# A macaron encoder block in float32r: 40 + 40 subtractions of the weight and activation splits put on GpSimd instead of VectorE

## The chip, the cores and the metric

The kernel runs on one core of a Trainium2 chip. Its engines work side by side, each through its own queue in order: TensorE (PE in the profile, its weight loads PEld), VectorE (DVE), ScalarE (ACT), GpSimd (POOL), and SyncE (SP), which here issues the DMAs. The metric is device time in microseconds, the median of several runs. The profile is one execution of its own.

## The reference, cut to what matters

One encoder layer over a sequence of 512 tokens with width 1024, all in float32: a feed-forward block, a mixer (gated convolution and mLSTM heads), and a second feed-forward block, each with a norm before and after and a residual. The two feed-forward blocks are what the change touches:

```python
def swiglu(x, w_in, w_out):
    gate, up = jnp.split(x @ w_in, 2, axis=-1)
    return (jax.nn.silu(gate) * up) @ w_out

h = swiglu(rmsnorm(x, norm_ffn1_pre[l]), w_ffn1_in[l], w_ffn1_out[l])
x = x + FFN_RESIDUAL_SCALE * rmsnorm(h, norm_ffn1_post[l])
```

`w_in` is 1024 x 5632 (gate and up factors of 2816 columns each), `w_out` 2816 x 1024.

## The kernel before, in words

**Splits.** TensorE multiplies in float32r, which keeps fewer bits than float32. So each operand is split in two: `hi`, a rounding cast made by ScalarE, and `lo`, the rest `src - hi`, a subtraction made by VectorE. Both lines are in the helper `split` (lines 292 and 294), so all splits of the kernel show up under these two lines and are told apart by tile names and shapes. `split` has a parameter `eng` for the engine of the subtraction, with VectorE as its default. A product takes three matmuls: hi x hi, hi x lo, lo x hi. In the kernel before, GpSimd forms the rests of only the first four weight tiles (`ON_POOL`).

**Seven products.** Both feed-forward projections use a scheme with seven products of half-size blocks in place of eight (with sums and differences of blocks formed first).

**In-projection.** The hidden columns go in 22 steps of 128 (`NF`), `j`. The first two (`PLAIN`) are done plainly, the other 20 by seven products. For such a step `w_pair` (from line 151 on; the additions are line 158) takes the two raw 128 x 1024 weight tiles of a step, gate `g` and up `u`, forms sums and differences in place, and splits four things: `g` (products 1 and 2), `s1` (product 5), the changed `g` (products 6 and 3) and the changed `u` (products 7 and 4). The last of these is the up factor's split. In `ffn` the products of a step are written in the order 1, 5, (4 of the step before), 6, 3, 2, 7; each is 12 matmuls of 256 columns (line 431). Three PSUM banks (`x`, `y`, `z`) hold a step's sums, and between the products ScalarE copies (lines 495 to 506) and VectorE adds (lines 503, 505, 508, 509 and 484) take them out: product 4 adds onto the bank that line 508 has read after product 7. `w_get(1)` keeps one step's weights formed ahead.

**Out-projection.** The 22 row blocks of `w_out` go in the order `OUT`: five groups "a" (`SEVEN` = 5), each over a pair of row blocks, then "b", "k", "b", "k" and so on, then the rest "k". A group "a" does products 1, 5, 6 and 7, a "b" products 2, 3 and 4 (line 564, 6 matmuls of 512 columns for each product), and a "k" is a plain row block (line 589, 24 matmuls).
- `w_out_a` prepares the right sides of an "a": three subtractions of 512 columns (line 191), a split of `r0` (1024 columns: products 1 and 7) and splits of `r1` and `t` (512 each: products 5 and 6).
- `left_a` prepares its left side from the hidden activations `h`: three additions of 256 columns (line 531) and splits of 256, 256 and 512 columns, the last of them for products 7 and 6.
- `w_out_b` and `left_b` do the same for a "b"; product 4's weight there is the split into the tile `wt` (subtraction before it: line 214).
- After the last "a", `taken` moves the sums out of PSUM (ScalarE copies at lines 574 and 576, VectorE additions at line 531), since the banks are used again.

**What sets the order.** The kernel is written in the Tile framework. A planner, which runs the instructions against a timeline of its own before the program is emitted, decides the order within each engine's queue, and inserts the waits. Instructions passed to `pin` keep their written order; in `ffn` that ends for the other engines after the first four plain products, and for TensorE after the first of the seven products. So from there the order of the products, the copies and the splits is the planner's.

**Buffers.** Twelve split tiles of 1024 columns (`wpool`, seven for a step of the in-projection, four for an "a"), four raw weight tiles (`rawp`) that the loads on SyncE's queue fill as they come free, 13 larger tiles (`big`) for activations, eight PSUM banks.

Of the kernel before, what the change touches and what calls it, by code (L numbers as in the profile page):

```python
# [37 lines left out]
def encoder_kernel(ctx: ExitStack, tc: tile.TileContext, a: dict, out: bass.AP):  # L38
    nc = tc.nc
# [14 lines left out]
    def nm(s):  # L54
        uid[0] += 1
        return f"{s}_{uid[0]}"
# [7 lines left out]
    def t2(dt=F32):  # L64
        return t2p.tile([P, 512], dt, tag="t2", name=nm("t2"))

    def t4(dt=F32):
        return t4p.tile([P, 1024], dt, tag="t4", name=nm("t4"))
# [4 lines left out]
    def f32(ap):  # L73
        return ap.bitcast(F32)
# [10 lines left out]
    def pin(ins):  # L85

        if pinned["PE" if ins.ins.engine == nc.tensor.engine else "rest"]:
            tc.keep_in_program_order(ins)
# [62 lines left out]
    def w_pair(g, u):  # L151


        def wt(n):
            return wpool.tile([P, 1024], F32R, tag="w", name=nm(n))

        def add(o, a_, b_, op):
            nc.vector.tensor_tensor(out=o, in0=a_, in1=b_, op=op)  # L158

        c = (slice(0, 512), slice(512, 1024))  # L160
        s1 = t2()
        add(s1, u[:, c[0]], u[:, c[1]], ALU.add)
        add(u[:, c[0]], g[:, c[0]], u[:, c[0]], ALU.subtract)
        gh, gl = wt("whi"), wt("wlo")
        split(gh, gl, g)
        add(g[:, c[0]], s1, g[:, c[0]], ALU.subtract)
        add(g[:, c[1]], g[:, c[1]], g[:, c[0]], ALU.subtract)
        s1w = wt("ws1")
        split(s1w[:, c[0]], s1w[:, c[1]], s1)
        ch_, cl = wt("whi"), wt("wlo")  # L170
        split(ch_, cl, g)
        uh, ul = wt("whi"), wt("wlo")
        split(uh, ul, u)

        def q(h_, l_, a_, b_):
            return tuple(v[:, r].rearrange("p (k f) -> p k f", k=KD // 2) for v, r in ((h_, a_), (l_, b_)))

        return {
            1: q(gh, gl, c[0], c[0]), 2: q(gh, gl, c[1], c[1]), 5: q(s1w, s1w, c[0], c[1]),
            6: q(ch_, cl, c[0], c[0]), 3: q(ch_, cl, c[1], c[1]),  # L180
            7: q(uh, ul, c[0], c[0]), 4: q(uh, ul, c[1], c[1]),
        }
# [3 lines left out]
    def w_out_a(r0, r1):  # L186

        c = (slice(0, 512), slice(512, 1024))

        def sub(o, a_, b_):  # L190
            nc.vector.tensor_tensor(out=o, in0=a_, in1=b_, op=ALU.subtract)

        def wt(n):
            return wpool.tile([P, 1024], F32R, tag="w", name=nm(n))

        sub(r1[:, c[0]], r0[:, c[1]], r0[:, c[0]])
        sub(r0[:, c[1]], r1[:, c[1]], r0[:, c[1]])
        t = t2()
        sub(t, r1[:, c[1]], r1[:, c[0]])
        kept.append(t)  # L200
        ah, al = wt("whi"), wt("wlo")
        split(ah, al, r0)
        bh, bl = wt("whi"), wt("wlo")
        split(bh[:, c[0]], bl[:, c[0]], r1[:, c[0]])
        split(bh[:, c[1]], bl[:, c[1]], t)
        return {1: (ah[:, c[0]], al[:, c[0]]), 7: (ah[:, c[1]], al[:, c[1]]),
                5: (bh[:, c[0]], bl[:, c[0]]), 6: (bh[:, c[1]], bl[:, c[1]])}

    def w_out_b(r1):

        c = (slice(0, 512), slice(512, 1024))
        hi, lo, t = (wpool.tile([P, 1024], F32R, tag="w", name=nm(n)) for n in ("whi", "wlo", "wt"))
        split(hi, lo, r1)
        nc.vector.tensor_tensor(out=r1[:, c[0]], in0=r1[:, c[0]], in1=kept.pop(0), op=ALU.subtract)
        split(t[:, c[0]], t[:, c[1]], r1[:, c[0]])
        return {2: (hi[:, c[0]], lo[:, c[0]]), 3: (hi[:, c[1]], lo[:, c[1]]), 4: (t[:, c[0]], t[:, c[1]])}

    def w_split(n):
        for _ in range(n):
            if not loaded:  # L220
                w_load(1)
            if not loaded:
                return
            raws, kk = loaded.pop(0)
            if isinstance(kk, str):
                ready.append((w_out_a if kk == "a" else w_out_b)(*raws))
                continue
            if len(raws) == 2:
                ready.append(w_pair(*raws))
                continue  # L230
            raw = raws[0]
            hi = wpool.tile([P, 1024], F32R, tag="w", name=nm("whi"))
            lo = wpool.tile([P, 1024], F32R, tag="w", name=nm("wlo"))
            eng = nc.gpsimd if done[0] in ON_POOL else nc.vector
            done[0] += 1
            split(hi, lo, raw, eng)
            if kk > 1:
                hi, lo = (v.rearrange("p (k f) -> p k f", k=kk) for v in (hi, lo))
            ready.append((hi, lo))
# [51 lines left out]
    def split(hi, lo, src, eng=nc.vector):  # L291
        latest["hi"] = nc.scalar.copy(out=hi, in_=src)  # L292
        pin(latest["hi"])
        latest["lo"] = eng.tensor_tensor(out=lo, in0=src, in1=f32(hi), op=ALU.subtract)  # L294
        pin(latest["lo"])
# [139 lines left out]
    def ffn(xq, between, finish, mid=None, within=None, ahead=(2, 2, 1, 1), late=None):  # L435
# [51 lines left out]
        for j in range(PLAIN, NF):  # L487
# [4 lines left out]
            a_, u, c = t2(), t2(), t2()  # L492
# [34 lines left out]
        def hcol(k):  # L527
            return h[k // 4][:, k % 4, 0:512]

        def tt(o, a_, b_, op):  # L530
            nc.vector.tensor_tensor(out=o, in0=a_, in1=b_, op=op)  # L531

        def halves():
            t = bigt(F32R).rearrange("p q f -> p (q f)")
            return t[:, 0:1024], t[:, 1024:2048]

        def parts(hi, lo, at):
            return {n: (hi[:, c:c + 256], lo[:, c:c + 256]) for n, c in at.items()}

        def left_a(i):  # L540
            a_, b_ = hcol(2 * i), hcol(2 * i + 1)
            hi, lo = halves()
            s1 = t4()[:, 0:256]
            tt(s1, a_[:, early], b_[:, early], ALU.add)
            split(hi[:, 0:256], lo[:, 0:256], a_[:, later])
            tt(a_[:, early], a_[:, later], a_[:, early], ALU.subtract)
            tt(a_[:, later], s1, a_[:, later], ALU.subtract)
            split(hi[:, 256:512], lo[:, 256:512], s1)
            split(hi[:, 512:1024], lo[:, 512:1024], a_)
            return parts(hi, lo, {1: 0, 5: 256, 7: 512, 6: 768})  # L550

        def left_b(i):
# [42 lines left out]
        for at, (kind, n) in enumerate(OUT):  # L595
            if kind == "k":
                if plain_n % 2 == 0:
                    hs = bigt(F32R)
                q = 2 * (plain_n % 2)
                plain_n += 1  # L600
                hT = (hs[:, q, 0:512], hs[:, q + 1, 0:512])
                split(hT[0], hT[1], hcol(n))
                ks[n] = (hT, w_get(min(2, len(OUT) - 1 - at)))
                if n == 12 and mid:
                    mid()
                if n < NF - TAIL:
                    for tb in range(NT):
                        for half in range(2):
                            mm_out(tb, half, n, *ks[n])
            elif kind == "a":  # L610
                left, right = left_a(n), w_get(1)
                for m in (1, 5, 6, 7):
                    product_out(m, left, right, n == 0, n == SEVEN - 1)
                    if n == SEVEN - 1:
                        taken(m)
            else:
                left, right = left_b(n), w_get(2)
                for m in (2, 3, 4):
                    product_out(m, left, right, n == 0 and m == 4, False)
# [339 lines left out]
    for tb in range(NT):  # L959
        pv_ = ps()  # L960
        n = 0
        for k in range(KD):
            hi, lo = wv[k // 2]
# [198 lines left out]
```

## Time and profile before

| | |
|---|---|
| median of 3 runs | 918.28 us (918.09 to 918.73) |
| the profiled execution | 915.36 us, span 913.7 us, granted TensorE clock 0.999 |
| PE busy | 900.1 us, 99% of the span |
| DVE busy | 716.2 us, 78% |
| ACT busy | 444.6 us, 49% |
| POOL busy | 44.7 us, 5% |
| DMA | 96.47 MB, mean 106 GB/s |

The first feed-forward block runs from the start to about 342 us (its in-projection to 228 us), the mixer to about 567 us, the second block from there to the end (its in-projection to 783 us). Busy time is an average over stages with different limits; a row of a group gives line, engine, operation, output tile and input tile, shape and count, then the busy time, the mean of one in ns, and the idle time ahead of it with what ended it. A row of the timeline or of the chain gives the start in us from the span's start and the duration. The matmuls' ends are modelled, so their pace is read from starts and counts, not from the duration of one.

### The profile page before, as it was taken

The page shows a single profiled execution, that of the slowest core. Times are in us where ns is not written, and L with a number is a line of the kernel's source. Part 1 is how long each engine was busy: PE and PEld are TensorE (multiplying, and loading weights), DVE is VectorE, ACT ScalarE, POOL GpSimd, SP SyncE. Part 2 cuts the span into 40 slices and gives each one's busy share as a digit, 9 for nine tenths or more (in the row PEclk, how much of TensorE's full clock was granted, in tenths as well). Part 3 has the DMA queues.
Part 4 walks back from the last instruction along what each step waited for, and adds up shares of the span by engine and source line. Part 5 has one row for each costly group of instructions (what it writes and reads, how often), then busy time and mean ns, then how long its engine had stood idle before and what let it go on. Part 6 is the DMA issues. An engine that isn't in the chain of part 4 may idle for free.

```text
span 913.7 us, 15022 instructions
## 1 busy us (share of the span) xinstructions
PE 900.1 (99%) x6015; PEld 816.7 (89%) x6015; DVE 716.2 (78%) x1196; ACT 444.6 (49%) x745; POOL 44.7 (5%) x67
## 2 busy tenths in 40 slices
PE   8999999999999999999999999999999999999997
PEld 7999999999877888987888888999999999977885
DVE  6988998888988359498787746889888988999435
ACT  6655555555456235452434335545545545566311
POOL 5000000000002001000011000000000000000000
PEclk9999999999999999999999999999999999999999
DMA  8233443343335614231422602224343432343402
GB/s 256 68 114 116 119 135 97 102 127 96 93 127 149 199 47 116 63 100 47 116 70 70 197 12 66 74 68 118 112 120 93 118 108 87 119 140 110 162 2 91
DMA packets 126257, 96.47 MB, mean 106 GB/s; under 512 B 4182, under 2 KB 114794, under 8 KB 126187
## 3 DMA queue, kind: packets, MB, share of 16 engines
q1 hardware_dynamic: 126186, 95.51, 35.1%
q8 instruction: 47, 0.77, 0.4%
q14 instruction: 24, 0.19, 0.1%
HBM read 93.40 MB, written 2.10 MB: 105 GB/s over the span
## 4 chain that ended last, share of the span: by engine, by line
PE 93%; DVE 4%; ACT 1%; issue 1%; DMA 1%; SPq 0%; POOL 0%; DVEq 0%; POOLq 0%; ACTq 0%
PE ps L431 43%; PE ps L589 13%; PE ps L422 12%; PE ps L564 9%; PE ps L453 5%; PE ps L1119 5%; PE ps L965 2%; DVE big L294 1%; DVE wlo L294 1%; PE ps L343 1%; DVE big L531 1%; PE ps L1035 1%; DMA x<-in_x_dram 1%; PE ps L983 0%; PE ps L391 0%
## 5 line engine op out<-in xcount | busy, mean ns | idle before, releaser
L294 DVE TENSOR_TENSOR wlo<-raw,whi 128x1024 fp32r<-128x1024 f32 x207 | 245.0, 1192 | 58.9 <-ACT whi L292 44.2
L292 ACT CAST whi<-raw 128x1024 fp32r<-128x1024 f32 x211 | 211.8, 1028 | 145.9 <-DVE raw L158 45.0
L431 PE MATMUL ps<-big,whi 128*128 128x256 f32 x1920 | 264.8, 280 | 0.0
L431 PEld LDWEIGHTS ps<-big,whi 128*128 128x128 f32 x1920 | 243.5, 188 | 0.5
L431 PE MATMUL ps<-big,wlo 128*128 128x256 f32 x960 | 150.9, 280 | 0.0
L431 PEld LDWEIGHTS ps<-big,wlo 128*128 128x128 f32 x960 | 129.3, 188 | 0.0
L589 PE MATMUL ps<-whi,big 128*128 128x512 f32 x384 | 121.9, 395 | 0.2 <-ACT whi L292 0.2
L589 PEld LDWEIGHTS ps<-whi,big 128*128 128x128 f32 x384 | 72.0, 188 | 17.4 <-ACT whi L292 0.6
L422 PE MATMUL ps<-big,whi 128*128 128x512 f32 (+1 forms) x384 | 79.8, 358 | 0.2 <-DVE den L1053 0.2
L564 PE MATMUL ps<-whi,big 128*128 128x512 f32 x240 | 75.9, 395 | 2.6 <-ACT big L292 2.6
L589 PE MATMUL ps<-wlo,big 128*128 128x512 f32 x192 | 75.6, 395 | 0.0
L422 PEld LDWEIGHTS ps<-big,whi 128*128 128x128 f32 x384 | 63.5, 188 | 11.2 <-PE ps L1077 0.4
L431 PE MATMUL ps<-big,ws 128*128 128x256 f32 x480 | 65.3, 280 | 0.0
L431 PEld LDWEIGHTS ps<-big,ws 128*128 128x128 f32 x480 | 60.3, 188 | 0.0
L564 PEld LDWEIGHTS ps<-whi,big 128*128 128x128 f32 x240 | 44.7, 188 | 13.4 <-ACT big L292 3.4
L501 ACT COPY t<-ps 128x256 f32<-128x256 f32 x40 | 14.9, 371 | 72.8 <-PE ps L431 72.7
L292 ACT CAST big<-big 128x512 fp32r<-128x512 f32 (+2 forms) x68 | 36.1, 582 | 23.2 <-DVE big L531 10.8
L564 PE MATMUL ps<-wlo,big 128*128 128x512 f32 x120 | 44.9, 393 | 0.0
L589 PEld LDWEIGHTS ps<-wlo,big 128*128 128x128 f32 x192 | 36.1, 188 | 8.4
L422 PE MATMUL ps<-big,wlo 128*128 128x512 f32 (+1 forms) x192 | 41.1, 356 | 0.0
L294 DVE TENSOR_TENSOR big<-big,big 128x512 fp32r<-128x512 f32 (+2 forms) x68 | 40.7, 634 | 0.1
L422 PEld LDWEIGHTS ps<-big,wlo 128*128 128x128 f32 x192 | 32.1, 188 | 5.5
(212 smaller groups left out, 1143.3 us busy)
## 6 DMA issues: line engine op xcount, KB each, us to landing
raw<-in_w_ffn_in_dram SPq DMA_DIRECT2D x88, 512.0 KB, 4.8
raw<-in_w_ffn_out_dram SPq DMA_DIRECT2D x44, 512.0 KB, 5.0
raw<-in_w_mix_in_dram SPq DMA_DIRECT2D x24, 512.0 KB, 4.5
raw<-in_w_mix_out_dram SPq DMA_DIRECT2D x8, 512.0 KB, 3.6
raw<-in_w_ffn_out_dram SPq DMA_DIRECT2D x10, 256.0 KB, 4.0
out_dram<-x SPq DMA_DIRECT2D x8, 256.0 KB, 2.0
x<-in_x_dram SPq DMA_DIRECT2D x4, 256.0 KB, 4.9
x<-in_x_dram SPq DMA_DIRECT2D x2, 512.0 KB
```

The source lines that it names most:

```text
L292: latest["hi"] = nc.scalar.copy(out=hi, in_=src)
L294: latest["lo"] = eng.tensor_tensor(out=lo, in0=src, in1=f32(hi), op=ALU.subtract)
L343: pin(nc.tensor.transpose(out=pt[:, blk(k)], in_=xs[:, blk(4 * b + k)], identity=ident))
L422: nc.tensor.matmul(o, ww[:, k, :], xk(xT, xx, k, sl), start=n == 0, stop=n == 3 * KD - 1)
L431: pin(nc.tensor.matmul(o, ww[:, k, :], x[xx][:, k, :], start=first and n == 0, stop=n == 11, skip_group_check=True))
L453: pin(nc.tensor.matmul(o, ww[:, k, :], xq_hl(xq, (k // 4, th))[xx][:, k % 4, :], start=n == 0, stop=n == 3 * KD - 1))
L501: nc.scalar.copy(a_[:, h1], x[:, h0])
L531: nc.vector.tensor_tensor(out=o, in0=a_, in1=b_, op=op)
L564: nc.tensor.matmul(acc[tb + t][half], left[n][x][:, blk(t)], right[n][y], start=first and x == y == 0, stop=last_ and x == 1, skip_group_c ...
L589: nc.tensor.matmul(acc[tb][half], hT[hh][:, blk(tb)], w[ww][:, blk(half, 512)], start=fresh and hh == ww == 0, stop=k == NF - 1 and hh == ...
L965: nc.tensor.matmul(pv_, xk(xT, xx, k, blk(tb)), ww[:, k % 2, :], start=n == 0, stop=n == 3 * KD - 1)
L1119: nc.tensor.matmul(acc[half], yy[yi][:, k % 4, blk(tb)], wmo[k][wi][:, blk(half, 512)], start=(n == 0 and yi == 0 and wi == 0), stop=(n == ...
```

## The change

Four places hand `nc.gpsimd` to `split`: the rest of the up factor in `w_pair` (1024 columns, 20 per block), the rests of the weights of products 5 and 6 in `w_out_a` (2 x 512 columns, 5 groups per block) and of product 4 in `w_out_b` (512 columns, 5 per block), and the rest of the left side of products 7 and 6 in `left_a` (512 columns, 5 per block). Over both blocks these are 40 subtractions of 1024 and 40 of 512 columns. Nothing else is edited; the planner runs anew.

```diff
@@ w_pair
         uh, ul = wt("whi"), wt("wlo")
-        split(uh, ul, u)
+        split(uh, ul, u, nc.gpsimd)
@@ w_out_a
         bh, bl = wt("whi"), wt("wlo")
-        split(bh[:, c[0]], bl[:, c[0]], r1[:, c[0]])
-        split(bh[:, c[1]], bl[:, c[1]], t)
+        split(bh[:, c[0]], bl[:, c[0]], r1[:, c[0]], nc.gpsimd)
+        split(bh[:, c[1]], bl[:, c[1]], t, nc.gpsimd)
@@ w_out_b
-        split(t[:, c[0]], t[:, c[1]], r1[:, c[0]])
+        split(t[:, c[0]], t[:, c[1]], r1[:, c[0]], nc.gpsimd)
@@ left_a
             split(hi[:, 256:512], lo[:, 256:512], s1)
-            split(hi[:, 512:1024], lo[:, 512:1024], a_)
+            split(hi[:, 512:1024], lo[:, 512:1024], a_, nc.gpsimd)
```

## Prediction

> **What bounds the kernel now.** I read the page first, then the busy time by stage, then what TensorE waited for, then VectorE's instructions in the stage that looked tight.
>
> ```profile
> span 913.7 us, 15022 instructions
> PE 900.1 (99%) x6015; PEld 816.7 (89%) x6015; DVE 716.2 (78%) x1196; ACT 444.6 (49%) x745; POOL 44.7 (5%) x67
> ```
> ```profile
> 36.00:228.00 192.00, 192.00 (x1634) 192.00 (x1633) 167.69 (x265) 101.45 (x162) 0.00 (x0) 1.00 0.38 110
> 219.80:258.70 38.90, 38.90 (x230) 34.23 (x229) 38.69 (x73) 21.38 (x39) 0.00 (x0) 1.00 0.44 133
> 777.10:815.00 37.90, 37.90 (x214) 32.84 (x214) 37.90 (x72) 21.27 (x40) 0.00 (x0) 1.00 0.44 136
> ```
> ```profile
> PE ps L564 <- ACT big L292: 2.6, 2, 1.3
> ...
> PE ps L564 <- ACT wt L292: 0.9, 1, 0.9
> PE ps L589 <- ACT whi L292: 0.2, 1, 0.2
> ```
> ```profile
> 36.40 192.10 PE ps L431 x1632
> ...
> 862.96 44.52 PE ps L589 x192
> ```
>
> The columns of the second fence are the window, its length, then the busy time (instructions) of PE, PEld, DVE, ACT and POOL, the granted clock, the DMA share and GB/s. The fourth is from the chain that ended last (start, length, count). TensorE is busy throughout 36 to 228 us (the first block's in-projection): 192.10 us for 1632 matmuls of 256 columns is 0.117 us each, and a matmul of 512 columns takes 44.52 / 192 = 0.232 us. VectorE is 87% busy there (167.69 of 192.00), idle 24.3 us; GpSimd does nothing. In the transition to the out-projection (219.8 to 258.7, and 777.1 to 815.0 in the second block) VectorE has no idle time at all, while TensorE is still fed. The third fence, the waits of TensorE (us in total, times, longest), holds all that it lost in the two feed-forward blocks after their start: 2.6 + 0.9 + 0.2 = 3.7 us. So the change can win little, and can lose wherever it makes VectorE or the new GpSimd pieces late.
>
> **What the change is made of.** It adds and removes no arithmetic: 40 subtractions of 1024 columns (the up factor of each of 20 pairs, two blocks) and, per block, 5 x 3 of 512 columns in the "a" groups (weights of products 5 and 6, left side of 6 and 7) and 5 of 512 in the "b" groups (weight of product 4) go from VectorE to GpSimd. ScalarE's rounding casts, DMAs and matmul counts stay. The durations:
>
> ```profile
> L294 POOL TENSOR_TENSOR wlo<-raw,whi 128x1024 fp32r<-128x1024 f32 x4 | 9.6, 2402 | 1.4 <-ACT whi L292 1.3
> ```
> ```profile
> L294 DVE TENSOR_TENSOR wlo<-raw,whi 128x1024 fp32r<-128x1024 f32 x8 | 9.7, 1217 | 0.6 <-ACT whi L292 0.6
> ...
> L294 DVE TENSOR_TENSOR wlo<-t,whi 128x512 fp32r<-128x512 f32 x5 | 3.4, 680 | 0.0
> L294 DVE TENSOR_TENSOR wlo<-raw,whi 128x512 fp32r<-128x512 f32 x5 | 3.4, 680 | 0.0
> L294 DVE TENSOR_TENSOR big<-big,big 128x512 fp32r<-128x512 f32 x5 | 3.4, 679 | 0.0
> ```
> ```profile
> 255.36 0.68 DVE L294 TENSOR_TENSOR wlo<-t,whi 128x512 fp32r<-128x512 f32 x1
> 255.96 0.68 DVE L294 TENSOR_TENSOR big<-big,big 128x512 fp32r<-128x512 f32 x1
> 256.56 1.22 DVE L294 TENSOR_TENSOR wlo<-raw,whi 128x1024 fp32r<-128x1024 f32 x1
> 257.70 0.41 DVE L531 TENSOR_TENSOR big<-big 128x256 f32<-128x256 f32 x1
> ...
> 261.40 1.29 DVE L531 TENSOR_TENSOR big<-ps,big 128x512 f32<-128x512 f32 x2 [2.69 <-PE ps L564]
> ```
>
> Of the second fence (VectorE in 219.8 to 258.7 us) the last three rows are the 15 subtractions of the "a" groups: all lie in the tight stretch. Back to back, VectorE starts the next instruction 0.60 us after one of 512 columns and 1.14 us after one of 1024 (third fence): that is what it is spared. GpSimd takes 2.40 us for 1024 columns; for 512 no row stands, and I estimate half, 1.20 us. If the two engines ran beside each other freely, VectorE would be spared 15 x 0.60 = 9.0 us per tight stretch. Whether they do is the question.
>
> **Do they run beside each other?** Three places say: only when VectorE reads PSUM.
>
> ```profile
> 10.38 4.93 POOL L294 TENSOR_TENSOR wlo<-raw,whi 128x1024 fp32r<-128x1024 f32 x2 [1.27 <-ACT whi L292]
> ```
> ```profile
> 10.47 2.48 DVE L294 TENSOR_TENSOR big<-ps,big 128x512 fp32r<-128x512 f32 x4
> ```
> ```profile
> 458.25 0.64 POOL L1018 TENSOR_SCALAR_AFFINE_SELECT t<-t 128x512 f32<-128x512 f32 x1 [14.08 <-ACT t L1016]
> ```
> ```profile
> 458.47 0.96 DVE L294 TENSOR_TENSOR big<-t,big 128x512 fp32r<-128x512 f32 x1
> ```
> ```profile
> 283.99 0.21 POOL L706 CAST big<-rawg 128x32 fp32r<-128x32 f32 x1 [12.82 <-DMA rawg<-in_w_mix_in_dram]
> ```
> ```profile
> 284.14 1.36 POOL L706 CAST big<-rawg 128x32 fp32r<-128x32 f32 x2
> ```
> ```profile
> 284.18 1.24 DVE L294 TENSOR_TENSOR wlo<-raw,whi 128x1024 fp32r<-128x1024 f32 x1 [0.26 <-ACT whi L292]
> ```
>
> At 10.38 us two GpSimd subtractions ran beside VectorE's, which read one operand from PSUM: four in 2.48 us, the usual 0.6 each. At 458.47 a VectorE subtraction with both operands in SBUF met a GpSimd instruction that began at 458.25: it took 0.96 instead of 0.68 us. GpSimd ended at 458.89; from there to VectorE's end (459.43) are 0.54 us, so VectorE stood still until GpSimd was done. The other way round, two GpSimd casts, of 0.21 us each when alone, ended only at 284.14 + 1.36 = 285.50, just after the VectorE subtraction of 284.18 to 285.42. The two take turns, a whole instruction each.
>
> [...]
>
> **The sum.** In the tight stretches VectorE works without a pause, so what counts is how long each GpSimd subtraction keeps it standing, against 0.60 us spared. Lower bound: it does not stand at all, -0.60 each. The 0.64 us row: +0.04. Upper: 1.20 us, +0.60. I take a hold of 1.20, since it is the same operation's row halved, and that 85% of it blocks:
>
> ```profile
> L484 DVE TENSOR_TENSOR big<-ps,t 128x256 f32<-128x256 f32 x3 | 1.2, 414 | 0.0
> ...
> L503 DVE TENSOR_TENSOR t<-ps,t 128x256 f32<-128x256 f32 x2 | 0.8, 418 | 0.2 <-PE ps L431 0.2
> ...
> L508 DVE TENSOR_TENSOR t<-ps,t 128x256 f32<-128x256 f32 x2 | 0.8, 414 | 0.0
> ...
> L505 DVE TENSOR_TENSOR t<-ps,t 128x256 f32<-128x256 f32 x1 | 0.4, 416 | 0.0
> ```
>
> These 8 instructions read PSUM and may run under a hold: 8 x 0.33 = 2.7 us of the 38.9 - 9.0 = 29.9 that stay, 9%; I round the free share up to 15% for holds that start while VectorE waits for something else. So 1.20 x 0.85 - 0.60 = +0.42 us each, 15 x 0.42 = +6.3 us of VectorE time per block.
>
> What of it reaches TensorE depends on its lead in the last "a" group:
>
> ```profile
> 260.89 1.09 PE L564 MATMUL ps<-whi,big 128*128 128x512 f32 x4
> ```
> ```profile
> 813.46 0.68 DVE L294 TENSOR_TENSOR big<-big,big 128x512 fp32r<-128x512 f32 x1
> ```
> ```profile
> 815.71 1.09 PE L564 MATMUL ps<-whi,big 128*128 128x512 f32 x4
> ```
>
> A group has 4 products x 6 = 24 matmuls, 5.57 us. In the first block the last one ends at 260.89 + 4 x 0.232 = 261.82, so it began at 256.25; VectorE finished its last left rest at 256.64 (255.96 + 0.68), which the second or third product needs (in its third matmul) at 258.1 or 259.5: a lead of 1.5 to 2.9, I take 2.2. In the second block it began at 811.07 and the rest was there at 814.14, for a third product's third matmul at 814.3: a lead of 0.2. So TensorE loses 6.3 - 2.2 = 4.1 and 6.3 - 0.2 = 6.1 us. VectorE's pause of 2.69 us at 261.40 does not help: it lies behind the group that came late, and the matching pause of the second block is shorter.
>
> The "b" groups: the first of them falls into the stretch right behind, where VectorE again has no pause; +0.42 in each block, 0.8 in all. The others cost nothing: a "b" with its "k" group holds 18 + 24 matmuls (9.7 us), about twice the VectorE work that goes with it; without that cover they would cost 8 x 0.42 = 3.4 us.
>
> ```profile
> raw<-in_w_ffn_in_dram SPq DMA_DIRECT2D x88, 512.0 KB, 4.8
> ```
>
> The up factors (a 2.40 us subtraction for 1.14 spared, every 84 x 0.117 = 9.8 us): 20 x (2.40 x 0.85 - 1.14) = +18 us of VectorE time in a 192 us stage that has 24.3 idle. I cost it at nothing: the two weight tiles of a pair are formed a whole pair ahead and the up rests are used by products 7 and 4, the last. Without that cover the bounds are 0 and 20 x (2.40 - 1.14) = 25 us per block. The raw tile is given back up to 2.4 us later, and SyncE's queue with the next load behind it; a load lands in 4.8 us (row above) of the 9.8, so it stays ahead. On GpSimd nothing urgent is queued behind the new work: a wait there holds back only the next subtraction, and the norm's powers come after the blocks. GpSimd's own load is 3 x 1.20 = 3.6 us per "a" group plus up to three waits of 0.6 for a VectorE instruction: 5.4 of TensorE's 5.57, so it is no cushion either.
>
> Sum: 4.1 + 6.1 + 0.8 = +11.0 us. The profiled execution took 915.36 us (its span 913.7 and 1.7 around it), 2.9 below the median of the runs, 918.28. 915.36 + 11.0 = 926.4; on the median, **929.3 us**.
>
> **The rivals.** (1) *Relief, faster.* GpSimd reads in short pieces and lets VectorE through; VectorE ends each tight stretch up to 9 us earlier and TensorE's waits of 3.7 us go. For it: a wait of 0.9 us in the second block has its cast behind VectorE's subtractions. Against: the two of 1.3 us follow casts queued behind ScalarE copies that wait for TensorE itself, and would stay. So -1.1 to -3.7, 914.6 to 917.2 us; it decides if less than half (0.60 / 1.20) of a hold blocks. Chance 0.17. (2) *No change.* Holds fall where VectorE waits anyway, or the planner, which orders each engine's queue, forms the "a" pieces earlier and takes up the stretch: 918.3 us. Against: the second block's lead of 0.2. Chance 0.18. (3) *The in-projection too.* VectorE, at up to (167.7 + 18) / 192 = 97%, falls behind by single holds and empties PSUM late; product 4 may only write after a sum of product 7 has been read. At 0.3 us for each of 38 inner pairs, +11.4 more: 940.7 us. Against: the lead of a whole pair. Chance 0.15.
>
> **How the numbers follow.** Forecast 0.50 (within 921 to 937: both blocks with 0.64 and with 1.20 us fully blocking), rivals as above. What a measurement of this kernel can tell from no change is about 0.2%, 1.8 us. Faster by more: most of rival 1, 0.13. Within: the rest of it, rival 2 and the lowest end of the forecast, 0.22. Slower: 0.65. The range leaves out the lower part of rival 1 and the upper half of rival 3: 915 to 941 us.
>
> **What would show it.** Right: VectorE instructions of 512 columns from SBUF with means well above 0.68 us around the transition; GpSimd about 96 + 48 us busier; new TensorE waits on line 564 released by GpSimd or VectorE, some 4 to 6 us per block; the in-projection still without waits. Wrong: VectorE's durations unchanged beside a busy GpSimd (rival 1), stretched durations but no TensorE wait (rival 2), or waits on line 431 (rival 3). A different order of products on TensorE could make any of these terms wrong.

## The result: 28 us slower, and the profile after

The changed kernel takes 946.21 us (median of 4 runs, 944.24 to 946.77) against 918.18 us for the kernel before: ratio 1.0302 (1.0284 to 1.0320). The prediction had the sign and the two engines' exclusion, 929.3 us, and a range up to 941: too little by 17 us. One of the ten runs of the control among the experiments (e12) took 979.98 us at a granted clock of 0.851 and does not enter its ratio.

The head of the page of the profile after, then its busy times by window (columns as in the prediction: length, PE, PEld, DVE, ACT, POOL, granted clock, DMA share, GB/s), then its longest waits of TensorE (us in total, times, longest):

```profile
span 942.5 us, 15253 instructions
PE 910.6 (97%) x6015; PEld 821.6 (87%) x6015; DVE 736.6 (78%) x1116; ACT 446.8 (47%) x745; POOL 231.9 (25%) x147
```
```profile
38.00:226.00 188.00, 186.24 (x1580) 185.77 (x1579) 167.67 (x236) 97.14 (x152) 45.73 (x19) 1.00 0.37 109
226.00:262.00 36.00, 32.15 (x182) 27.17 (x181) 34.80 (x51) 17.49 (x33) 24.49 (x12) 0.95 0.33 103
262.00:292.00 30.00, 26.09 (x111) 20.64 (x112) 27.68 (x34) 18.47 (x33) 20.22 (x8) 1.00 0.33 100
593.00:795.00 202.00, 201.03 (x1706) 200.62 (x1705) 180.10 (x246) 108.81 (x168) 49.72 (x20) 1.00 0.35 101
795.00:836.00 41.00, 33.99 (x181) 27.67 (x180) 38.75 (x52) 17.11 (x33) 24.31 (x15) 1.00 0.35 107
836.00:870.00 34.00, 28.35 (x113) 22.31 (x112) 25.87 (x39) 20.92 (x37) 15.98 (x4) 0.90 0.31 103
```
```profile
PE ps L564 <- POOL wt L294: 5.6, 2, 4.5
PE ps L564 <- ACT big L292: 4.0, 3, 1.7
PE ps L564 <- DVE wlo L294: 4.0, 2, 2.6
PE ps L564 <- DVE t L503: 3.7, 2, 3.1
PE ps L431 <- DVE t L508: 2.2, 3, 1.2
PE ps L564 <- DVE big L484: 1.9, 1, 1.9
...
PE ps L564 <- POOL big L294: 1.2, 1, 1.2
```

Three things are to be seen. VectorE gave up 80 subtractions and is busier than before, 736.6 against 716.2 us: it stands still inside other instructions (line 158's 40 of `t<-raw` take 1176 ns each on the mean, 684 in the profile before). TensorE's losses lie in the two transitions to the out-projection: in the second and third window it is idle 3.9 + 3.9 us, in the last two 7.0 + 5.7 us; the in-projections lose 1.8 and 1.0. And its clock fell below 1.00 in two of the windows, which no window of the two blocks had before.

The waits name the new releasers: GpSimd itself (`wt`, product 4's weight, and `big`, the left side), and VectorE, late. The moved subtractions on GpSimd, from the groups of the profile after by shape:

```profile
L294 POOL TENSOR_TENSOR wlo<-raw,whi 128x1024 fp32r<-128x1024 f32 x44 | 109.9, 2497 | 313.1 <-ACT whi L292 222.0 <-DVE wlo L294 49.5 <-PE ps L431 41.7
L294 POOL TENSOR_TENSOR wt<-raw,wt 128x512 fp32r<-128x512 f32 x10 | 33.1, 3309 | 35.8 <-ACT wt L292 35.8
L294 POOL TENSOR_TENSOR big<-big,big 128x512 fp32r<-128x512 f32 x10 | 23.8, 2395 | 21.1 <-ACT big L292 21.1
L294 POOL TENSOR_TENSOR wlo<-raw,whi 128x512 fp32r<-128x512 f32 x10 | 15.8, 1582 | 7.6 <-ACT t L495 4.4 <-ACT whi L292 2.6 <-PE ps L564 0.6
L294 POOL TENSOR_TENSOR wlo<-t,whi 128x512 fp32r<-128x512 f32 x10 | 15.5, 1549 | 0.0
```

The same operation on 512 columns takes 1.55 us on the mean in one place and 3.31 in another. The worst of them, from the timelines of GpSimd, VectorE and TensorE:

```profile
846.04 12.77 POOL L294 TENSOR_TENSOR wt<-raw,wt 128x512 fp32r<-128x512 f32 x1 [7.19 <-ACT wt L292]
```
```profile
845.55 0.69 DVE L531 TENSOR_TENSOR big<-big,big 128x512 f32<-128x512 f32 x1
846.15 1.03 DVE L294 TENSOR_TENSOR big<-big,big 128x512 fp32r<-128x512 f32 x2
...
855.78 1.90 DVE L294 TENSOR_TENSOR big<-big,big 128x512 fp32r<-128x512 f32 x3
```
```profile
853.98 0.39 PE L564 MATMUL ps<-wt,big 128*128 128x512 f32 x1
858.86 2.50 PE L564 MATMUL ps<-wt,big 128*128 128x512 f32 x5 [4.49 <-POOL wt L294]
```

GpSimd's subtraction became ready at 846.04. VectorE then issued 19 instructions with both operands in SBUF without a pause, up to 857.68, and GpSimd ended at 858.81, 1.13 us after the last of them: it got no turn at any of the boundaries between them. TensorE waited for it for 4.49 us. And when it went on, five matmuls took 2.50 us, about half their usual pace: the clock. The windows around the two places where that happened:

```profile
241.80:245.20 3.40, 0.38 (x2) 0.00 (x0) 3.40 (x5) 0.00 (x0) 2.44 (x2) 1.00 0.21 77
245.20:248.70 3.50, 3.45 (x9) 2.66 (x10) 3.50 (x8) 2.24 (x5) 0.50 (x1) 0.54 0.00 0
...
854.00:858.80 4.80, 0.37 (x2) 0.00 (x0) 3.69 (x7) 1.14 (x2) 4.80 (x1) 0.76 0.00 0
858.80:863.20 4.40, 4.34 (x10) 3.46 (x11) 1.15 (x2) 1.81 (x4) 0.07 (x2) 0.50 0.69 235
```

The two stalls, from one matmul's start to the next, are 3.46 us (to 245.25) and 4.88 us (to 858.86). After them TensorE ran 3.4 and 4.4 us at half clock, one matmul of 512 columns every 0.427 us in place of 0.232. The clock does not fall at the same point: cut finer, it reads 1.00 up to 245.48 us, just after the first stall, but in the second it is 1.00 up to 856.4 and 0.50 from 856.5 to 863.2, so that there it fell in the middle of the stall. In the two places 19 matmuls start so slowly, which costs 3.8 us in all.

Of the 28.8 us between the two profiled spans, 10.9 lie in the first block, 15.3 in the second, 0.2 in the mixer, and 2.4 before the first weight matmul (line 453, at 13.69 us; at 11.28 in the profile before). The last is hardly an effect of the change: in seven of the experiments' profiles (e1 to e6 and e9) that matmul stands between 13.69 and 13.70, in four between 13.1 and 13.6 and in one (e7) at 11.39, whatever they moved.

### The profile page after: what moved, and what is told of

Read it like the earlier page. It is cut to its first block, busy times and chain, and to the rows that moved or that the text cites. A ratio compares the mean times of both kernels' runs of the same rounds, so it can differ in the third digit from the quotient of the medians.

```text
span 942.5 us, 15253 instructions
## 1 busy us (share of the span) xinstructions
PE 910.6 (97%) x6015; PEld 821.6 (87%) x6015; DVE 736.6 (78%) x1116; ACT 446.8 (47%) x745; POOL 231.9 (25%) x147
## 4 chain that ended last, share of the span: by engine, by line
PE 69%; DVE 14%; POOL 3%; ACT 3%; issue 2%; DMA 0%; DVEq 0%; POOLq 0%; ACTq 0%
PE ps L431 31%; PE ps L589 13%; PE ps L422 12%; PE ps L1119 5%; PE ps L564 3%; DVE wlo L294 3%; PE ps L965 2%; POOL wt L294 2%; DVE big L294 2%; DVE big L531 1%; DVE raw L158 1%; ACT whi L292 1%; ACT big L292 1%; PE ps L453 1%; POOL big L294 1%
## 5 line engine op out<-in xcount | busy, mean ns | idle before, releaser
L294 DVE TENSOR_TENSOR wlo<-raw,whi 128x1024 fp32r<-128x1024 f32 x157 | 221.2, 1413 | 96.5 <-ACT whi L292 78.0
L294 POOL TENSOR_TENSOR wlo<-raw,whi 128x1024 fp32r<-128x1024 f32 (+1 forms) x54 | 125.7, 2327 | 320.7 <-ACT whi L292 224.6
L431 PEld LDWEIGHTS ps<-big,wlo 128*128 128x128 f32 x960 | 129.3, 188 | 0.0
L589 PE MATMUL ps<-whi,big 128*128 128x512 f32 x384 | 122.9, 397 | 0.0
L564 PE MATMUL ps<-whi,big 128*128 128x512 f32 x240 | 79.3, 402 | 10.8 <-ACT big L292 4.0
L589 PE MATMUL ps<-wlo,big 128*128 128x512 f32 x192 | 76.4, 398 | 0.0
L310 POOL TENSOR_TENSOR rs<-rs,nhalf 128x1 f32<-128x1 f32 x24 | 13.6, 569 | 187.4 <-DVE rs L306 178.6
L564 PE MATMUL ps<-wlo,big 128*128 128x512 f32 x120 | 48.0, 402 | 4.0 <-DVE wlo L294 4.0
L158 DVE TENSOR_TENSOR t<-raw 128x512 f32<-128x512 f32 x40 | 47.0, 1176 | 0.0
```

What stands on the lines that cost most here:

```text
L310: nc.gpsimd.tensor_tensor(out=r[:, 0:w], in0=acc, in1=nhalf[:, 0:w], op=ALU.pow)
L431: pin(nc.tensor.matmul(o, ww[:, k, :], x[xx][:, k, :], start=first and n == 0, stop=n == 11, skip_group_check=True))
L564: nc.tensor.matmul(acc[tb + t][half], left[n][x][:, blk(t)], right[n][y], start=first and x == y == 0, stop=last_ and x == 1, skip_group_c ...
L589: nc.tensor.matmul(acc[tb][half], hT[hh][:, blk(tb)], w[ww][:, blk(half, 512)], start=fresh and hh == ww == 0, stop=k == NF - 1 and hh == ...
```

## The experiments

Theories. *Port*: VectorE's instructions with two SBUF operands and GpSimd's reading ones exclude each other, and the price is VectorE's standing plus GpSimd's waiting ("port" is only a name: the rows show the exclusion, not what makes it). *Order*: the planner, given other engines, put out another order of the queues, and that costs the time. *Relief* (rival 1 of the prediction) is answered on the way.

**Is it the port at all? Only writing on GpSimd.** (The diffs here and below show the main lines only.)

```diff
     def split(hi, lo, src, eng=nc.vector):
         latest["hi"] = nc.scalar.copy(out=hi, in_=src)
+        if eng is nc.gpsimd and not real[0]:
+            for _ in range(3):
+                nc.gpsimd.memset(f32(lo), 0.0)
+            return
```

> All moved subtractions are replaced on GpSimd by three memsets of the same piece (zeros: those rests are left out of the computation), so GpSimd is about as long busy but only writes SBUF. Port theory (VectorE with two SBUF inputs and GpSimd reading SBUF take turns, and the late pieces cost the time): VectorE's durations stay at 0.68 and 1.22 us, no wait of TensorE for GpSimd, 912 to 919 us. Order theory (the planner's new order of the queues costs the time, the port does not matter): still 935 us or more.

912.11 us, ratio 0.9940 (0.9925 to 0.9954): faster than before by 5.6 us. GpSimd was busy about as long (groups below), VectorE kept its 1.22 us, and what is left of TensorE's waits has nothing of the feed-forward blocks but 0.2 us at the second block's start (line 460). All waits of TensorE that this run shows, then two groups of GpSimd and one of VectorE:

```profile
PE ps L287 <- POOL warm L280: 1.3, 1, 1.3
PE ps L398 <- DVE t L390: 1.0, 1, 1.0
PE ps L429 <- DVE den L1060: 0.2, 1, 0.2
PE ps L460 <- ACT big L294: 0.2, 1, 0.2
```
```profile
L298 POOL MEMSET wlo<- 128x1024 f32 x120 | 114.8, 957 | 289.7 <-PE ps L438 178.4 <-ACT whi L294 80.3 <-PE ps L460 20.2
L298 POOL MEMSET wlo<- 128x512 f32 x60 | 29.4, 526 | 20.0 <-PE ps L571 10.6 <-PE ps L438 9.5
```
```profile
L301 DVE TENSOR_TENSOR wlo<-raw,whi 128x1024 fp32r<-128x1024 f32 x157 | 191.2, 1221 | 125.9 <-ACT whi L294 68.1 <-PE ps L438 22.1 <-ACT t L508 15.6
```

So with GpSimd pieces that only write, the move is worth 5.6 us, and between writing and reading lie 34 us. The order theory does not stand as it was put: the planner ran anew here too, on nearly the same split of work, and nothing was lost. (The memsets need no result of the cast, so they can begin earlier and the order is not the same as in the changed kernel; a run with its very order and no reading was not made. How much of the 34 us is due to that is open.)

**Which parts cost it?** Each part alone, by leaving `nc.gpsimd` out of the other calls of `split`:

```diff
+split(t[..], t[..], r1[..], nc.gpsimd)     # e2, in w_out_b
+split(uh, ul, u, nc.gpsimd)                # e3, in w_pair
+split(bh[..], bl[..], r1[..], nc.gpsimd)   # e5, in w_out_a
+split(bh[..], bl[..], t, nc.gpsimd)        # e5, in w_out_a
+split(hi[..], lo[..], a_, nc.gpsimd)       # e6, in left_a
```

> Only product 4's weight rest (512 columns, 5 per block) on GpSimd. Port theory with a GpSimd that gets no turn while VectorE issues back to back: one or two of these rests per block take 5 to 13 us and TensorE waits for them, +4 to +10 us, 922 to 928 us. Port theory with a turn after each VectorE instruction (as predicted): +0.8 us, 919 us. Order theory: nothing to be seen, 918 us.

> Only the up factors' rests (1024 columns, 20 per block) on GpSimd. Port theory: VectorE loses about 0.2 us net per pair, hidden but for the first pairs of each block, where TensorE waits about 1.5 us; +2 to +5 us, 920 to 923 us. If the in-projection's fuller VectorE also starts the out-projection's pieces late: +8 us or more, 926 us.

> Only the weight rests of products 5 and 6 (10 of 512 columns per block) on GpSimd. Holds alone: VectorE loses 1.15 - 0.60 = 0.55 us each, 5.5 us per block, less the lead of 2.2 and 0.2: +8 to +9 us, 926 us. Where GpSimd gets its turn at once or runs beside VectorE instructions that read PSUM, less: 920 us. If late pieces of GpSimd add to it: 930 us or more.

> Only the left rests of products 7 and 6 (5 of 512 columns per block) on GpSimd. Holds alone: 5 x 0.55 = 2.8 us per block, less the lead: +0.6 and +2.6, 921 us. With late pieces (a rest that waits out a back-to-back row of VectorE, and the group b behind it that overwrites what it reads): +5 us or more, 923 us or more.

| part on GpSimd | us | the kernel before beside it | ratio (95% interval) | us more |
|---|---|---|---|---|
| product 4's weight (e2) | 923.94 | 917.74 | 1.0066 (1.0051 to 1.0082) | 6.2 |
| up factors (e3) | 922.66 | 917.74 | 1.0052 (1.0033 to 1.0071) | 4.9 |
| weights of products 5 and 6 (e5) | 929.83 | 917.52 | 1.0132 (1.0117 to 1.0147) | 12.3 |
| left side of products 7 and 6 (e6) | 923.32 | 917.52 | 1.0063 (1.0048 to 1.0078) | 5.8 |

The sum is 29.2 us; the whole costs 28.0. The parts add up, which an accident of the planner's order would hardly do. The two smallest parts (e2 and e6), ten subtractions of 512 columns each, cost 6.2 and 5.8 us, about what they had cost VectorE (10 x 0.60). In e3 TensorE waits in early pairs of each block: 1.0 and 0.6 us for VectorE's line 508 at 73.7 and 84.6 us in the first, 0.4 for line 508 and 0.5 for ScalarE's line 495 at 620.7 and 630.8 us in the second. Up to there VectorE has hardly a pause (2.4 us idle in 36 to 90 us, 6.7 in the kernel before); the long in-projection behind these pairs shows no wait. In e5 the weights' own pieces are late:

```profile
PE ps L564 <- POOL wlo L294: 5.9, 4, 2.1
```

**Do they add up inside the whole?** Everything but product 4's weight, and the group "a" parts together:

> The whole change without product 4's weight, which stays on VectorE. If that part costs the same inside the whole as alone (6.2 us): 940 us. If its two long waits of the changed kernel's trace, with the half clock behind one of them, go in full: 937 us. If the time only moves to another wait: 945 us.

> The two parts of the group a together, without the up factors and product 4. If the parts add up: 946.2 - 4.9 - 6.2 = 935 us. If they cost more together (GpSimd's pieces queue behind one another): above the sum of the two runs beside this one; if they share one lead of TensorE, below it.

Without product 4's weight 938.02 us (ratio 1.0225, 1.0208 to 1.0242): that part costs 8.2 us in the whole, between the two first expectations and far from the third. The "a" parts together: 936.52 us (1.0200, 1.0183 to 1.0217), 19.0 us against 12.3 + 5.8 = 18.1 apart. They neither share a lead nor pile up much.

**When does GpSimd get a turn?** Test rows of VectorE subtractions appended behind the kernel before (in outline):

```diff
+    for i in range(24):   # sink <- x3 - x2, 512 columns, back to back
+        pin(nc.vector.tensor_tensor(out=sink[:, i % 4, 0:512], in0=x3[:, 0:512], in1=x2[:, 0:512], op=ALU.subtract))
+    # ahead of the row VectorE writes 8 columns (the gate); beside it on GpSimd:
+    # an 8-column copy of the gate, then the instruction tried
```

> The kernel before with a test row appended behind its last stage: 24 VectorE subtractions of 512 columns back to back, and beside them one GpSimd instruction. Turn after each VectorE instruction: a GpSimd subtraction of 512 columns takes at most 1.3 + 0.7 = 2.0 us. No turn in a back-to-back row: it takes as long as the row, some 14 us, while beside VectorE instructions that read PSUM it takes 1.3 us and a memset is not delayed. The 32-column ones, which ended at each boundary in the kernel before, tell whether a small one gets through. The whole run some 90 us above the kernel before, which means nothing.

The timeline of GpSimd in these rows:

```profile
914.27 1.74 POOL L1156 TENSOR_TENSOR big<-x,x 128x512 f32<-128x512 f32 x1
...
929.49 1.29 POOL L1156 TENSOR_TENSOR big<-x,x 128x512 f32<-128x512 f32 x1
...
943.76 14.43 POOL L1148 COPY big<-big 128x8 f32<-128x8 f32 x1 [12.85 <-DVE big L1147]
...
959.54 2.68 POOL L1156 TENSOR_TENSOR big<-x,x 128x32 f32<-128x32 f32 x4
```

Both expectations hold in places. In the first row the subtraction got its turn after one VectorE instruction (1.74 us), beside PSUM reads it took 1.29, and the four 32-column ones went through boundary by boundary. But in the row that began at 943.62, right behind another and without a pause, a copy of only 8 columns, which comes ahead of the subtraction in question, waited 14.43 us, until the row was over; the same happened in the fifth row. Size did not decide it here: 8 columns were kept out, 512 had been let in. Ahead of the fourth and the sixth row, which let GpSimd in, VectorE had stood waiting for GpSimd (0.62 and 0.76 us). Ahead of the first it had not, but for a gap of 0.04 us two instructions earlier, so why GpSimd got in there is open. The second probe puts the request into the course of a row, with something in its middle:

```diff
+    vrow(8); pin(nc.vector.tensor_copy(gsrc[:, 0, 0:8], x3[:, 0:8]))      # releases GpSimd
+    pin(nc.gpsimd.tensor_tensor(out=pk.., in0=gsrc[:, 0, 0:512], in1=x2.., op=ALU.subtract))
+    vrow(8); opener(); vrow(8)
```

> Again rows of VectorE subtractions appended behind the kernel before, each with one GpSimd subtraction of 512 columns asked for in its course, and in its middle something that may let it in: nothing; an instruction that reads PSUM (512 columns, 8 columns); a memset of 8 columns; a one-input instruction of 512; a wait for ScalarE; then rows of 256 and of 128 columns with nothing. [...] If a pause is needed: only the wait lets it in. If chance decides: no pattern. The time of the whole means nothing.

GpSimd's eight requests in order (nothing; PSUM 512; PSUM 8; memset of 8; one input of 512; the wait for ScalarE; rows of 256; rows of 128):

```profile
919.23 15.33 POOL L1148 TENSOR_TENSOR big<-big,x 128x512 f32<-128x512 f32 x1 [7.63 <-DVE big L1147]
934.84 1.63 POOL L1148 TENSOR_TENSOR big<-big,x 128x512 f32<-128x512 f32 x1 [0.28 <-DVE big L1147]
951.03 5.85 POOL L1148 TENSOR_TENSOR big<-big,x 128x512 f32<-128x512 f32 x1 [14.55 <-DVE big L1147]
966.61 5.85 POOL L1148 TENSOR_TENSOR big<-big,x 128x512 f32<-128x512 f32 x1 [9.74 <-DVE big L1147]
982.20 15.82 POOL L1148 TENSOR_TENSOR big<-big,x 128x512 f32<-128x512 f32 x1 [9.74 <-DVE big L1147]
998.30 1.63 POOL L1148 TENSOR_TENSOR big<-big,x 128x512 f32<-128x512 f32 x1 [0.28 <-DVE big L1147]
1015.26 6.40 POOL L1148 TENSOR_TENSOR big<-big,x 128x512 f32<-128x512 f32 x1 [15.32 <-DVE big L1147]
1032.07 13.97 POOL L1148 TENSOR_TENSOR big<-big,x 128x512 f32<-128x512 f32 x1 [10.41 <-DVE big L1147]
```

With nothing, GpSimd waited out the whole row. An instruction of 8 columns that reads PSUM, and a VectorE memset of 8 columns, both let it in exactly there (5.85 us). A one-input instruction of 512 columns from SBUF did not (15.82). The second and the sixth request do not test their openers: VectorE had waited for GpSimd right ahead of them (the 15 us of the request before), and GpSimd got in at the first boundary, as in the first probe. In the rows of 256 it got in at the seam of the two rows, where two instructions in a row write the same tile and the trace has a gap of 0.03 us between VectorE's instructions, which elsewhere in the row overlap by 0.08; that the gap did it was not tried. The rows of 128 have no such gap, and GpSimd waited for their end. The openings that worked were both short; a memset of more columns was not tried, while PSUM reads of 512 let GpSimd in in the first probe. What decides between "at the first boundary" and "not at all" stays open. What these rows and the 12.77 us show is that a running row without an opening can keep GpSimd out up to its end (15.33 us), and that it got in where VectorE had waited (1.63 us) or an opening came (5.85 us).

**Does the waiting make the loss in the kernel?** Openings put into it: a VectorE memset of 8 columns, which let GpSimd in in e9 (5.85 us in place of 15.33), behind each of VectorE's split subtractions in the out-projection. In e10 only product 4's weight rest is on GpSimd, the part that costs 6.2 us alone; e11 is the whole change, e12 the kernel before.

```diff
+        if door[0] is not None and eng is nc.vector:
+            with tc.issue_after(latest["lo"].ins):
+                nc.vector.memset(door[0], 0.0)
```

> [...] If the long wait for a turn is what this part costs (6.2 us): no rest takes more than 3 us, +1 to +2.5 us, 920 us. If the hold of 1.15 us is what costs: unchanged, 924 us.

> The whole change with the same memsets. If late pieces of GpSimd make up the part of the loss that the prediction had not: about 12 us back, 932 to 936 us. If VectorE's stretched time alone makes the loss: 945 us or more, since openings only let GpSimd in more often.

> Control: the kernel before with the same memsets and nothing moved. They cost VectorE 77 x 0.07 = 5 us over both blocks where it is busy all the time: 918 to 921 us by every theory; a value above that has to be taken off the other two.

The control costs nothing measurable: 917.83 us, 1.0004 (0.9995 to 1.0014). With product 4's weight on GpSimd the openings bring 923.94 down to 919.17 us (1.0021, 1.0010 to 1.0033): 1.5 us above the kernel before beside it in place of 6.2, so 4.7 of the 6.2 us go with the wait for a turn. The whole change comes down to 938.46 us (1.0228, 1.0213 to 1.0243): 20.8 us above the kernel before beside it in place of 28.0, so 7.2 us better, less than the 12 expected and more than the other theory allowed. The durations of product 4's weight rest (min/median/max in ns), in the changed kernel and with the openings:

```profile
L294 POOL TENSOR_TENSOR wt<-raw,wt x10: 1292/1302/12768, 271.1 to 874.6; 128x512 fp32r<-128x512 f32 x10
```
```profile
L294 POOL TENSOR_TENSOR wt<-raw,wt x10: 1295/1341/1742, 272.0 to 872.2; 128x512 fp32r<-128x512 f32 x10
```

None is late any more, and no wait of TensorE for GpSimd is left. What remains are mostly waits for VectorE, the longest of them here (the edit moves lines: 568, 434 and 511 are 564, 431 and 508 of the other kernels):

```profile
PE ps L568 <- DVE wlo L294: 5.4, 2, 4.0
PE ps L434 <- DVE t L511: 4.0, 4, 2.0
```

In the changed kernel VectorE stands while GpSimd reads (1176 in place of 684 ns for `t<-raw`); the waits suggest that it still does with the openings, but no row of e11 here shows it. Two stretches of half clock remain as well, some 3.1 us.

No version here beats the kernel before except the first, which leaves the rests out.

## Why the prediction was wrong

*The port, and VectorE's standing: right in kind; its size fits the first block's transition, where it was worked out, and is too large elsewhere.* The prediction had +0.42 us for each moved subtraction of 512 columns, +6.3 per block. In the profile after, VectorE's two-operand subtractions and additions run 16.8 us over their usual durations in 226 to 292 us, for 17 moved ones that had cost 17 x 0.60 = 10.2: +6.6 us; in 795 to 870 it is 14.6 - 19 x 0.60 = +3.2. That is 0.99 and 0.77 us of standing for each moved one, 82 and 64% of a hold of 1.2 us, where the prediction took 85%. In the in-projections some 24 and 27 us of standing fall on 19 and 20 moved subtractions, 1.3 us each or about half of 2.40: VectorE lost only some 3 and 4 us net there, where the prediction had 18. Two groups show who stands:

```profile
L191 DVE TENSOR_TENSOR t<-raw 128x512 f32<-128x512 f32 x5 | 5.0, 993 | 0.0
...
L531 DVE TENSOR_TENSOR big<-big 128x256 f32<-128x256 f32 x7 | 6.0, 878 | 1.2 <-POOL big L294 1.2
```

(VectorE in 226 to 262 us: 0.99 in place of 0.68 us, 0.88 in place of 0.41.) The hold, 0.64 us in the prediction's row, is longer here: VectorE ends only after GpSimd. For 512 columns: GpSimd's subtraction of 231.84 takes 1.47 us, up to 233.31, and VectorE's split subtraction of 256 columns at 232.08 takes 1.51 us in place of 0.41, up to 233.59. For 1024 columns, on GpSimd and VectorE:

```profile
78.30 2.50 POOL L294 TENSOR_TENSOR wlo<-raw,whi 128x1024 fp32r<-128x1024 f32 x1 [6.61 <-ACT whi L292]
```
```profile
78.87 2.48 DVE L158 TENSOR_TENSOR t<-raw 128x512 f32<-128x512 f32 x1
```

VectorE's instruction takes 2.48 in place of 0.68 us and ends at 81.35, 0.55 us after GpSimd's end at 80.80.

*"Up to three waits of 0.6 for a VectorE instruction": the step that failed.* It took GpSimd to get its turn at the next boundary, from the casts at 284 us of the profile before. Those had just seen VectorE wait (0.26 us for ScalarE in the row quoted there). In a running row GpSimd can be kept waiting for the row's end or an opening: 12.77 us at 846. So GpSimd's pieces are late by themselves, and not only by what VectorE loses.

*The "b" groups at 0.8 us: the term most mis-sized.* Alone they cost 6.2, in the whole 8.2. The prediction found VectorE without a pause there and counted the hold only; in the whole GpSimd was kept out in just such a stretch (12.77 us for a pass of 1.30); alone the longest piece took 5.73.

*The up factors "at nothing": wrong by 4.9 us.* The lead of a whole pair covers most pairs, and rival 3, which put 0.3 us on each of 38, came in four early pairs only: TensorE waited there on line 431, for line 508 three times, 2.6 us in all in e3. The rest in e3's profile is at the beginning of the first block's out-projection: a wait for ScalarE's cast of 1.9 us, 1.3 in the kernel before, and a stretch of half clock behind it, some 1.5 us.

*The group "a": 4.1 + 6.1 expected, 19.0 measured (e8).* In that run's profile TensorE waits 5.5 us for GpSimd's pieces (2.9 for `big`, 2.6 for `wlo`) and loses another 5.7 to half clock; the prediction had neither. Its path, TensorE waiting for VectorE in the transitions, is there too: in the profile of the whole change these waits are 9.6 us (4.0 + 3.7 + 1.9 in the rows above). The prediction had no term for the clock at all: it took a stall to cost its own length.

*What is left open.* The forecast was 17 us short. About 7 of them go when GpSimd is let in (28.0 to 20.8). The other ten stay with the openings: the up factors (4.9 alone) and the half clock are in them, but these overlap, and they were not taken apart further.

*Relief, rival 1, "-1.1 to -3.7": wrong here, since GpSimd's reads do hold VectorE up, but also too small as a bound.* With GpSimd only writing, e1, the gain is 5.6 us, and the two waits of 1.3 us "behind ScalarE copies that would stay" are gone as well: a freer VectorE lets the planner place those copies better or earlier, which of the two was not tried.

*The time itself.* The sum was made against a profiled execution 2.9 us below the median. In its trace the first weight matmul stands 2.4 us earlier than in most others, which fits that correction.

## What to carry to other kernels

Moving a two-operand elementwise instruction from a busy VectorE to GpSimd relieved nobody here, where VectorE's own instructions have both operands in SBUF: GpSimd's slower pass (1.29 us for 512 columns beside PSUM reads in e4, against VectorE's 0.68) became largely VectorE's (82 and 64% of 1.2 us in the two transitions), and where VectorE issued without a pause GpSimd's piece could come as late as VectorE's next stop (12.77 us). Before such a move, look for the stretch where VectorE has no idle time and read there which of its instructions read PSUM; give GpSimd what only writes (e1, 5.6 us faster than before), or what nobody needs soon. After some of TensorE's stalls half clock came on top: about 1.5 us after a pause of 2.33 us in e3, 1.5 in each of the two stretches of e11, 3.8 us for the two places of the changed kernel; after 3.58 us in e2 there was none.

## What the runs showed of the hardware that was not expected

- GpSimd was kept waiting through a whole row of VectorE instructions: 12.77 us for a pass of 1.3 (the changed kernel), 14.43 us for 8 columns, 15.33 and 15.82 us for 512 (the probes). A memset or a PSUM read of 8 columns on VectorE ended it (5.85 us).
- TensorE's clock halved after some stalls: 0.427 us for 512 columns in place of 0.232, for 3.4 and 4.4 us of matmuls in the changed kernel. It was down for 3.4 us in the first place (245.48 to 248.9 us) and for 6.8 in the second (856.4 to 863.2), at 0.50 in both. The stalls' length alone does not decide: in e3 the matmuls paused for 2.33 us from one start to the next at 266.04 us, and those from 269.18 to 272.15 went at half pace, while in e5 a pause of 2.68 us at 267.77 and in e2 one of 3.58 us at 837.09 had no such consequence. What decides is not shown.
